# Which engine does which split: part of the GpSimd work of a two-layer encoder given to VectorE and ScalarE

## The chip, the core and the metric

The kernel runs on one core of a Trainium2 chip. Its engines are TensorE (PE in the profile), VectorE (DVE), ScalarE (ACT), GpSimd (POOL) and SyncE (SP), which issues all the DMAs here. The metric is the device time of one execution in microseconds (us).

## The reference

A prompt of 1024 tokens and a sample of 512 tokens, each of width 1024, go through two layers. Layer 0 projects x into eight pieces. Two of them (xa, za) go through a pooling mixer with windows of 2, 4, 8 and 16 tokens. The others go through a convolution and, per head, through a chunkwise mLSTM in both directions. Layer 1 is attention with grouped keys and an output gate. Each layer ends with an output projection and a layer norm.

```python
# pooling mixer, group g of 128 channels, window w
mean = (cs[hi] - cs[lo]) / cnt                       # cs: running sum over time
mixed = einsum('btc,cd->btd', mean - xa, w_pool[g]);  out_a = mixed * pool_scale * silu(za)
# mLSTM, one chunk of 128 tokens, per head and direction
s   = (q @ k.T) * exp(dmat - m_row)                  # dmat: masked decays
num = s @ v + ex * (C @ q);   den = s.sum(-1) + ex * (n @ q)
h   = num / max(abs(den), exp(-m_row))
C   = decay * C + einsum('s,sv,sk->vk', ws, v, k)    # ws: weight of each token for the state
n   = decay * n + einsum('s,sk->k', ws, k)
# layer 1
o = softmax(q @ k.T * scale) @ v;  x = layer_norm(ALPHA * x + (o * silu(z)) @ w_out)
```

All is in float32.

## The kernel before

**Split products.** A float32 matrix product is made of three matmuls in a shorter type (float32r). Each operand is split into a high part `h` (the value rounded to that type) and a low part `l` (the value less `h`), and PE sums h x h, h x l and l x h. The high part is a copy or cast, by ScalarE (`hi_act`, line 96) or by GpSimd (`hi_pool`, line 93). The low part is a subtraction, by VectorE (`lo_dve`, line 99) or, in `split_light`, by GpSimd (line 103). Since these helpers record the instructions, many groups of the profile carry lines 93, 96, 99 and 103, and the tile's name tells what is split.

**Order.** The program is written as Python generators that are merged, and the framework then orders each engine's instructions by a simulated timeline. Every engine, and SP's queue of DMAs, works its list off in order. So a store that waits for its data holds back every DMA behind it in SP's queue.

**Layer 0's token projections** (`layer0`, lines 285 to 338). Two pieces of the weights (`wt`) are multiplied with the tokens, for three groups of 512 tokens: the prompt's two and the sample's one. Each group makes four tiles `ev`, which ScalarE copies out of PSUM (line 322, or with a tanh in line 325) into a ring `th` of the pool `st` (three buffers), and which SP then stores. Between the groups runs `weight_sums`: for ten blocks of layer 1's weights, four pieces are loaded into a ring `sr` of eight buffers, four differences are made (line 1120), two on GpSimd and two on VectorE, each in the place of one of its inputs, and the differences are stored. They are read again in layer 1. Two rounds of table products (line 1132) follow. Here too stand the gates: VectorE's scans over time (lines 467 to 470), and transposes of the gates on PE into tiles `ct` (`gate_cols`, line 507), which need PSUM banks that the copies of `ev` set free.

**The heads** (from line 339). Periods overlap for the heads of prompt and sample: `early` prepares a head, `chains` runs the state from chunk to chunk, `head_fin` finishes it, and `fill` runs the projections of the heads to come (`proj_g`, with weights from `wunit`). 16 blocks of weights in two units each are split for the prompt; the split weights are stored and loaded again for the sample. In `wunit` the flag `wlight` chooses `split_light`. In `early`, line 643 multiplies the values `v` with the state's token weights `ws` into `vw`, which is split into `vwh` and `vwl` for the matmuls `U`. GpSimd also masks the decays (line 606) and takes the powers for the norms (line 195). `pool_mix` builds a window's sum by doublings (line 817), one to four additions in a row. `out_weights` splits the sixteen tiles of layer 0's output weights (`wo0`), every other one by `split_light`.

**After the heads** come layer 0's output projection with its norm (`mid`), layer 1's projections and attention, with a hand-written order on PE.

Of the kernel before, what the change touches and what calls it, by code (L numbers as in the profile page):

```python
# [10 lines left out]
F32 = mybir.dt.float32  # L11
F32R = mybir.dt.float32r
AF = mybir.ActivationFunctionType
ALU = mybir.AluOpType
# [4 lines left out]
P = 128  # L19
# [37 lines left out]
class Kern:  # L57
# [217 lines left out]
    def layer0(self, seqs):  # L275
# [4 lines left out]
        with ExitStack() as ctx:  # L280
# [4 lines left out]
            with ExitStack() as c1:  # L285
                mp = c1.enter_context(tc.tile_pool(name="mm0", bufs=4, space=PSUM, reuse_waits="tile"))
                mq = c1.enter_context(tc.tile_pool(name="ms0", bufs=4, space=PSUM, reuse_waits="tile"))
                gp = c1.enter_context(tc.tile_pool(name="gate", bufs=1, reuse_waits="tile"))
                xq = c1.enter_context(tc.tile_pool(name="x0b", bufs=1, reuse_waits="tile"))
                st = c1.enter_context(tc.tile_pool(name="st0", bufs=3, reuse_waits="tile"))  # L290
                self.wp = c1.enter_context(tc.tile_pool(name="w0", bufs=1, reuse_waits="tile"))
                self.wbufs, self.rbufs = 10, 4
                presums = self.weight_sums(st)
                self.gate_places(gp)

                acc = mq.tile([P, 512], F32, tag="ms", name="warm")
                for i in range(10):
                    self.mm(acc[:, 0:512], self.wgh[:, 0, :], self.wgh[:, 0:4, :], True, True)
                for piece in range(2):
                    units = []  # L300
                    for gi, (s, g) in enumerate(groups):
                        xh, xl = x0[s]
                        pool, tag = ((mp, "mm"), (mq, "ms"))[gi % 2]
                        acc = [pool.tile([P, 512], F32, tag=tag, name=f"t{s}{piece}{g}{i}") for i in range(4)]
                        for k in range(KD):
                            if gi == 0:
                                units.append(self.wunit(a["w0t"][piece, k], f"wt{piece}{k}"))
                            if piece == 0:
                                self.load_x(s, k, g, xh, xl, xp if s == first else xq, st)
                            elif gi and k == 3:  # L310
                                self.gate_cols(seqs[gi - 1], *gates[gi - 1], mq if pool is mp else mp, "ms" if pool is mp else "mm")
                            wh, wl = units[k]
                            for i in range(4):
                                c = slice(i * P, (i + 1) * P)
                                self.mm(acc[i], xh[k][g][:, c], wh, k == 0, False)
                                self.mm(acc[i], xh[k][g][:, c], wl, False, False)
                                self.mm(acc[i], xl[k][g][:, c], wh, False, k == KD - 1)
                        for i in range(4):
                            n = 4 * g + i
                            t = st.tile([P, 512], F32, tag="th", name=f"ev{s}{piece}{n}")  # L320
                            if piece == 0:
                                nc.scalar.copy(t, acc[i])
                                self.load(self.vd[s][n], t)
                            else:
                                nc.scalar.activation(t, acc[i], AF.Tanh, scale=0.5)
                                self.load(self.thd[s][n], t)
                        if piece == 0 and gi == 0:
                            self.consts0a()
                            self.gate_weights(gp)
                            self.consts0b(mq)  # L330
                        if piece or gi:
                            for _ in range(4 if piece and gi == len(groups) - 1 else 2):
                                next(presums, None)
                    if piece == 0:
                        gates = [self.gates(s, *x0[s], gp, mq) for s in seqs]
                        for k in range(KD):
                            for x, X in enumerate(x0[seqs[1]]):
                                self.load(self.xsd[k, x], X[k][0].bitcast(F32))
# [4 lines left out]
            self.rings = {"mm": (pp, 2), "me": (pp, 3), "mx": (pp, 1), "mc": (pp, 2)}  # L343
            self.wp = c2.enter_context(tc.tile_pool(name="w1", bufs=1, reuse_waits="tile"))
            self.wbufs, self.rbufs = 4, 2
            self.wlight = True
            hp = self.hp = c2.enter_context(tc.tile_pool(name="hd", bufs=1, reuse_waits="tile"))
            self.xbt, self.state = {}, {}

# [34 lines left out]
            for i in range(-1, n + 1):  # L384
# [16 lines left out]
                    ts = self.mid_early[i + 2 - len(plan)]  # L401
                    jobs.append((chain(*[self.mid_tile(t) for t in ts]), 16 * len(ts)))
                merge(*jobs)
            self.wlight = False

    def head_plan(self, seqs):

# [143 lines left out]
    def early(self, s, h, hp, hf):  # L551
# [25 lines left out]
        for g in range(NG):  # L577
# [3 lines left out]
            kl = hp.tile([P, 512], F32R, tag="kl", name=f"kl{s}{h}{g}")  # L581
            N, keep = vs[g]
            qh, ql = keep[:, 0, :], keep[:, 1, :]
            self.hi_pool(kh, xc)
            self.lo_dve(kl, xc, kh)
            yield
            wh, wl = self.wsm["wqk"]
# [31 lines left out]
            nc.gpsimd.memset(v[:, :, P:130], 1.0)  # L619
            vh = hf.tile([P, 4, 130], F32R, tag="vh", name=f"vh{s}{h}{g}", bufs=1)  # L620
            vl = hf.tile([P, 4, P], F32R, tag="vl", name=f"vl{s}{h}{g}", bufs=1)
            self.hi_pool(vh, v)
            self.lo_dve(vl, v[:, :, 0:P], vh[:, :, 0:P])
            yield
            ps = self.bank("me", f"S{s}{h}{g}")
# [12 lines left out]
            for i in range(0, 4, 2):  # L638
# [1 line left out]
                vw = hf.tile([P, 2, 2, 130], F32, tag="vw", name=f"vw{s}{h}{g}{i}")  # L640
                vb = v[:, i:i + 2, :].unsqueeze(2).to_broadcast([P, 2, 2, 130])
                ws = col["ws"][:, 4 * g + i:4 * g + i + 2, :, h:h + 1].to_broadcast([P, 2, 2, 130])
                nc.gpsimd.tensor_tensor(out=vw, in0=vb, in1=ws, op=ALU.mult)
                vwh = hf.tile([P, 2, 2, 130], F32R, tag="vwh", name=f"vwh{s}{h}{g}{i}")
                vwl = hf.tile([P, 2, 2, 130], F32R, tag="vwl", name=f"vwl{s}{h}{g}{i}")
                self.hi_act(vwh, vw)
# [153 lines left out]
    def pool_mix(self, s, gi, hp):  # L800
# [10 lines left out]
        for g in range(NG):  # L811
            gc = slice(g * 512, (g + 1) * 512)
            cur, ln, step = xa[:, g * 512:g * 512 + 512 + w - 1], 512 + w - 1, 1
            for i in range(gi + 1):
                nxt = hp.tile([P, 526], F32, tag=f"y{i % 2}", name=f"y{s}{gi}{g}{i}")
                ln -= step
                nc.gpsimd.tensor_tensor(out=nxt[:, 0:ln], in0=cur[:, 0:ln], in1=cur[:, step:step + ln], op=ALU.add)
                cur, step = nxt, step * 2
            if g == 0:
                nc.vector.tensor_tensor(out=cur[:, 0:left], in0=cur[:, 0:left], in1=self.edge[:, gi, 0:left], op=ALU.mult)  # L820
# [5 lines left out]
            sz = self.load_z(s, gi, g, hp)  # L826
            qh = hp.tile([P, 512], F32R, tag="zs", name=f"plh{s}{gi}{g}", bufs=2)
            ql = hp.tile([P, 512], F32R, tag="zs", name=f"pll{s}{gi}{g}", bufs=2)
            self.hi_pool(qh, cur[:, 0:512])
            self.lo_dve(ql, cur[:, 0:512], qh)  # L830
            yield
            ps = self.bank("mx", f"mx{s}{gi}{g}")
# [21 lines left out]
    def out_weights(self, wn, half):  # L854

        wh, wl = [], []
        for k in range(KD):
            l = self.x0p.tile([P, 512], F32R, tag=f"xl{k}{1 - half}", name=f"{wn}l{half}{k}")
            h = self.x0p.tile([P, 512], F32R, tag=f"xh{k}{1 - half}", name=f"{wn}h{half}{k}")
            raw = self.hp.tile([P, 512], F32, tag="zs", name=f"{wn}r{half}{k}", bufs=2)  # L860
            self.load(raw, self.a[wn][k, :, half * 512:(half + 1) * 512])
            if k % 2:
                self.split_light(h, l, raw)
            else:
                self.hi_act(h, raw)
                self.lo_dve(l, raw, h)
            wh.append(h)
            wl.append(l)
        self.wo[half] = (wh, wl)
# [237 lines left out]
    def weight_sums(self, pool):  # L1107

        nc = self.nc
        for kind, n in (("q", 4), ("z", 4), ("kv", 2)):
            for k in range(n):
                r = {}
                for h, j in ((0, 0), (0, 1), (1, 1), (1, 0)):
                    t = r[h, j] = pool.tile([P, 512], F32, tag="sr", name=f"sr{kind}{k}{h}{j}", bufs=8)
                    self.load(t.rearrange("p (k n) -> p k n", k=2) if kind == "kv" else t, self.piece(kind, k, h, j))
                for o, e, x, y, d in ((0, nc.gpsimd, (0, 1), (0, 0), (0, 0)), (2, nc.vector, (1, 1), (0, 1), (0, 1)),
                                      (1, nc.gpsimd, (1, 1), (0, 0), (1, 1)), (3, nc.vector, (1, 1), (1, 0), (1, 0))):
                    e.tensor_tensor(out=r[d], in0=r[x], in1=r[y], op=ALU.subtract)  # L1120
                    self.load(self.sums[kind][k, o], r[d])
                yield
        g = pool.tile([P, 4, P], F32, tag="sr", name="srg", bufs=8)
        self.load(g.rearrange("p a f -> p (a f)"), self.a["g4"].partition_broadcast(P))
        for h in range(2):
            ns = slice(4 * h, 4 * h + 4)
            for i, n in enumerate(("cos", "sin")):
                t = pool.tile([P, 4, P], F32, tag="sr", name=f"srt{h}{n}", bufs=8)
                self.load(t, self.a[n][:, ns, :])
                for w in range(2):  # L1130
                    o = pool.tile([P, 4, P], F32, tag="sr", name=f"sro{h}{n}{w}", bufs=8) if w == 0 else t
                    nc.vector.tensor_tensor(out=o, in0=t, in1=g[:, 2 * w + i:2 * w + i + 1, :].to_broadcast([P, 4, P]), op=ALU.mult)
                    self.load(self.tabd[w][i][:, ns, :], o)
            yield
# [519 lines left out]
```

## Time and profile before

| | |
|---|---|
| median of three runs | 1479.44 us (1478.56 to 1479.59) |
| the profiled execution | 1477.55 us, of which the span of the instructions is 1475.8 us |
| granted PE clock over the span | 0.99 |
| bytes read and written in HBM | 155.94 and 86.03 MB |

A row of windows gives a stretch, and for each engine its busy time and how many instructions ran in it; then the granted clock of PE as a share of the full one, the busy share of the 16 DMA engines, and GB/s. A row of waits names who waited for whom, the sum, how often, and the longest, all in us. A row of a group gives the instruction's line, engine, operation, `out<-in`, shapes and count, then its busy time in us and the mean of one in ns, then the idle time of the engine ahead of it and what ended that. A row in time begins with the start and the duration in us. Names ending in p belong to the prompt, those ending in s to the sample. The stages by time: token projections 0 to 165 us, heads 165 to about 640, output projection to 711, layer 1 to the end.

### The profile page before, as it was taken

The page shows a single profiled execution, that of the slowest core. Times are in us where ns is not written, and L with a number is a line of the kernel's source. Part 1 is how long each engine was busy: PE and PEld are TensorE (multiplying, and loading weights), DVE is VectorE, ACT ScalarE, POOL GpSimd, SP SyncE. Part 2 cuts the span into 40 slices and gives each one's busy share as a digit, 9 for nine tenths or more (in the row PEclk, how much of TensorE's full clock was granted, in tenths as well). Part 3 has the DMA queues.
Part 4 walks back from the last instruction along what each step waited for, and adds up shares of the span by engine and source line. Part 5 has one row for each costly group of instructions (what it writes and reads, how often), then busy time and mean ns, then how long its engine had stood idle before and what let it go on. Part 6 is the DMA issues. An engine that isn't in the chain of part 4 may idle for free.

```text
span 1475.8 us, 21781 instructions
## 1 busy us (share of the span) xinstructions
PE 1435.2 (97%) x7190; PEld 1189.3 (81%) x7190; DVE 1012.5 (69%) x1976; ACT 738.4 (50%) x1666; POOL 609.0 (41%) x616
## 2 busy tenths in 40 slices
PE   9998999999999999999999999999999999999997
PEld 7876888878787788788888789888878888888886
DVE  6584156585777878877779548555677777777675
ACT  3341355454545555445346545557755555555551
POOL 5431334353542333659426002432345545444641
PEclk9998999999999999999999999999999999999999
DMA  9976564555597776545554876345321111111311
GB/s 311 396 282 235 190 201 139 204 176 178 160 310 245 233 229 208 181 147 185 172 167 145 271 226 234 121 136 157 114 72 58 57 51 37 43 58 58 100 51 57
DMA packets 181586, 243.42 MB, mean 165 GB/s; under 512 B 14673, under 2 KB 90193, under 8 KB 181473
## 3 DMA queue, kind: packets, MB, share of 16 engines
q1 hardware_dynamic: 181472, 242.03, 49.7%
q8 instruction: 57, 0.93, 0.3%
q14 instruction: 57, 0.46, 0.1%
HBM read 155.94 MB, written 86.03 MB: 164 GB/s over the span
## 4 chain that ended last, share of the span: by engine, by line
PE 65%; DVE 13%; DMA 12%; issue 4%; ACT 3%; POOL 2%; SPq 1%; DVEq 0%; ACTq 0%; POOLq 0%
PE Sp L106 6%; PE Op L106 6%; PE o1p L106 6%; PE ptp L1442 4%; PE o1s L106 3%; PE qs L106 3%; PE o0s L106 3%; PE z L106 3%; PE zp L106 3%; PE o0p L106 3%; PE xbp L106 2%; PE kvs L106 2%; PE ts L106 1%; PE Ss L106 1%; PE z4P L106 1%
## 5 line engine op out<-in xcount | busy, mean ns | idle before, releaser
L1420 POOL TENSOR_SCALAR prp<-prp,smp 128x1024 f32<-128x1024 f32 x64 | 73.3, 1145 | 137.8 <-DVE smp L1419 112.7
L96 ACT CAST pwp<-ptp 128x512 fp32r<-128x512 f32 x128 | 74.8, 585 | 92.1 <-PE ptp L1442 91.4
L106 PE MATMUL Op<-pwp,Vhp 128*128 128x512 f32 x256 | 109.0, 426 | 0.6 <-DVE pwp L99 0.6
L99 DVE TENSOR_TENSOR pwp<-ptp,pwp 128x512 fp32r<-128x512 f32 x128 | 87.2, 682 | 22.9 <-ACT pwp L96 22.7
L1415 ACT ACTIVATE prp<-Sp,nbp,rqp 128x1024 f32<-128x1024 f32 (+1 forms) x68 | 78.8, 1159 | 21.6 <-DVE nbp L1412 15.8
L1407 DVE TENSOR_REDUCE nbp<-Sp 128x1 f32<-128x1024 f32 (+1 forms) x68 | 78.4, 1153 | 11.8 <-PE Sp L106 11.7
L1442 PEld LDWEIGHTS ptp<-idn,prp 128*128 128x128 f32 x512 | 63.5, 140 | 20.0 <-DVE pwp L99 1.9
L1442 PE MATMUL ptp<-idn,prp 128*128 128x128 f32 x512 | 77.0, 272 | 2.0 <-POOL prp L1420 1.4
L106 PEld LDWEIGHTS Op<-pwp,Vhp 128*128 128x128 f32 x256 | 48.3, 189 | 8.0 <-DVE pwp L99 1.0
L106 PE MATMUL tp<-wt_l,xhp 128*128 128x512 f32 x128 | 51.2, 404 | 0.0
L106 PE MATMUL tp<-wt_h,xlp 128*128 128x512 f32 x128 | 51.1, 403 | 0.0
L106 PE MATMUL o0p<-wo0l,ah0p 128*128 128x512 f32 x128 | 50.8, 399 | 0.2 <-DVE wo0l L99 0.2
L106 PE MATMUL o0p<-wo0h,ah0p 128*128 128x512 f32 x128 | 50.6, 397 | 0.2 <-ACT wo0h L96 0.2
L106 PE MATMUL tp<-wt_h,xhp 128*128 128x512 f32 x128 | 50.7, 403 | 0.0
L106 PE MATMUL o0p<-wo0h,al0p 128*128 128x512 f32 x128 | 50.3, 394 | 0.0
L106 PE MATMUL Op<-pwp,Vlp 128*128 128x512 f32 x128 | 50.1, 391 | 0.0
L1067 POOL TENSOR_TENSOR rskp<-sskp,mhalf 128x2 f32<-128x2 f32 x8 | 7.0, 879 | 100.2 <-DVE sskp L1063 100.2
L106 PE MATMUL Sp<-Khp,qhp 128*128 128x512 f32 x128 | 41.9, 403 | 0.0
L106 PE MATMUL o1p<-wo,ah1p 128*128 128x512 f32 x128 | 40.7, 399 | 0.0
L106 PE MATMUL Sp<-Klp,qhp 128*128 128x512 f32 x128 | 40.7, 393 | 0.0
L106 PE MATMUL Sp<-Khp,qlp 128*128 128x512 f32 x128 | 40.4, 391 | 0.0
L699 DVE SCALAR_TENSOR_TENSOR Usp<-Usp,decbp 128x130 f32<-128x130 f32 x48 | 22.2, 462 | 25.8 <-ACT Usp L656 25.2
(1150 smaller groups left out, 4999.5 us busy)
## 6 DMA issues: line engine op xcount, KB each, us to landing
wt_r<-w0t SPq DMA_DIRECT2D x16, 256.0 KB, 5.2
xrp<-xT_p SPq DMA_DIRECT2D x16, 256.0 KB, 5.4
srq<-w1q SPq DMA_DIRECT2D x16, 256.0 KB, 5.4
sum_q<-srq SPq DMA_DIRECT2D x16, 256.0 KB, 5.3
srz<-w1z SPq DMA_DIRECT2D x16, 256.0 KB, 5.1
sum_z<-srz SPq DMA_DIRECT2D x16, 256.0 KB, 4.8
wp<-rd_p SPq DMA_DIRECT2D x16, 256.0 KB, 4.9
z_p<-zsp SPq DMA_DIRECT2D x16, 256.0 KB, 3.2
```

Source lines behind the costliest of these rows:

```text
L96: self.nc.scalar.copy(out, in_)
L99: self.nc.vector.tensor_tensor(out=out, in0=in_, in1=hi.bitcast(F32), op=ALU.subtract)
L106: self.nc.tensor.matmul(out, lhsT=lhsT, rhs=rhs, start=start, stop=stop)
L699: nc.vector.scalar_tensor_tensor(out=U[:, i, :], in0=U[:, i + o, :], scalar=dec[:, 4 * d + h, n:n + 1], in1=U[:, i, :], op0=ALU.mult, op1= ...
L1067: nc.gpsimd.tensor_tensor(out=rs[:, 0:nh], in0=ss[:, 0:nh], in1=self.mhalf[:, 0:nh], op=ALU.pow)
L1407: nc.vector.tensor_reduce(out=nb[:, i:i + 1], in_=b, op=ALU.max, axis=AX.X, negate=True)
L1415: nc.scalar.activation(pr[:, i * W:(i + 1) * W], b, AF.Exp, bias=nb[:, 0:1], scale=rq, accum_out=sm[:, i:i + 1])
L1420: nc.gpsimd.tensor_scalar(pr, pr, sm, 0.0, ALU.mult, ALU.add)
L1442: nc.tensor.transpose(pt[:, h * P:(h + 1) * P], prs[h][:, c * P:(c + 1) * P], self.idn)
```

## The change

Four things. In layer 0 the ring `th` gets four buffers, the ring `sr` seven, and all four differences of a weight block are made by VectorE. In the heads the weights' low parts go from GpSimd to VectorE (`wlight` stays off, and `hi_w` is ScalarE, which makes the high parts as before). The weighted values `vw` and the windows' sums go from GpSimd to VectorE; so do the low parts of every other tile of `wo0`. The high parts of the keys' input (`kh`), the values (`vh`) and the pooled tiles (`plh`) go from GpSimd to ScalarE. GpSimd keeps the masks, the powers and the memsets in the heads. `hi_w` is set back after the heads, so what follows is not edited.

```diff
@@ layer0
-  t = st.tile([P, 512], F32, tag="th", name=f"ev{s}{piece}{n}")
+  t = st.tile([P, 512], F32, tag="th", name=f"ev{s}{piece}{n}", bufs=4)
...
-  self.wlight = True
+  self.hi_w = self.hi_act
...
-  self.wlight = False
+  self.hi_w = self.hi_pool
@@ early
-  self.hi_pool(kh, xc)
+  self.hi_act(kh, xc)
...
-  self.hi_pool(vh, v)
+  self.hi_act(vh, v)
...
-  nc.gpsimd.tensor_tensor(out=vw, in0=vb, in1=ws, op=ALU.mult)
+  nc.vector.tensor_tensor(out=vw, in0=vb, in1=ws, op=ALU.mult)
@@ pool_mix
-  nc.gpsimd.tensor_tensor(out=nxt[:, 0:ln], in0=cur[:, 0:ln], in1=cur[:, step:step + ln], op=ALU.add)
+  nc.vector.tensor_tensor(out=nxt[:, 0:ln], in0=cur[:, 0:ln], in1=cur[:, step:step + ln], op=ALU.add)
...
-  self.hi_pool(qh, cur[:, 0:512])
+  self.hi_act(qh, cur[:, 0:512])
@@ out_weights
-  if k % 2:
-      self.split_light(h, l, raw)
-  else:
-      self.hi_act(h, raw)
-      self.lo_dve(l, raw, h)
+  self.hi_act(h, raw)
+  self.lo_dve(l, raw, h)
@@ weight_sums: every tile of the ring "sr"
-  bufs=8
+  bufs=7
...
-  for o, e, x, y, d in ((0, nc.gpsimd, (0, 1), (0, 0), (0, 0)), (2, nc.vector, (1, 1), (0, 1), (0, 1)),
-                        (1, nc.gpsimd, (1, 1), (0, 0), (1, 1)), (3, nc.vector, (1, 1), (1, 0), (1, 0))):
-      e.tensor_tensor(out=r[d], in0=r[x], in1=r[y], op=ALU.subtract)
+  for o, x, y, d in ((0, (0, 1), (0, 0), (0, 0)), (2, (1, 1), (0, 1), (0, 1)),
+                     (1, (1, 1), (0, 0), (1, 1)), (3, (1, 1), (1, 0), (1, 0))):
+      nc.vector.tensor_tensor(out=r[d], in0=r[x], in1=r[y], op=ALU.subtract)
```

More of the change, by code (lines that the diff above doesn't have):

```diff
@@ L1115, in weight_sums @@
                 for h, j in ((0, 0), (0, 1), (1, 1), (1, 0)):
-                    t = r[h, j] = pool.tile([P, 512], F32, tag="sr", name=f"sr{kind}{k}{h}{j}", bufs=8)
+                    t = r[h, j] = pool.tile([P, 512], F32, tag="sr", name=f"sr{kind}{k}{h}{j}", bufs=7)
                     self.load(t.rearrange("p (k n) -> p k n", k=2) if kind == "kv" else t, self.piece(kind, k, h, j))
-                for o, e, x, y, d in ((0, nc.gpsimd, (0, 1), (0, 0), (0, 0)), (2, nc.vector, (1, 1), (0, 1), (0, 1)),
-                                      (1, nc.gpsimd, (1, 1), (0, 0), (1, 1)), (3, nc.vector, (1, 1), (1, 0), (1, 0))):
-                    e.tensor_tensor(out=r[d], in0=r[x], in1=r[y], op=ALU.subtract)
+                for o, x, y, d in ((0, (0, 1), (0, 0), (0, 0)), (2, (1, 1), (0, 1), (0, 1)),
+                                   (1, (1, 1), (0, 0), (1, 1)), (3, (1, 1), (1, 0), (1, 0))):
+                    nc.vector.tensor_tensor(out=r[d], in0=r[x], in1=r[y], op=ALU.subtract)
                     self.load(self.sums[kind][k, o], r[d])
                 yield
-        g = pool.tile([P, 4, P], F32, tag="sr", name="srg", bufs=8)
+        g = pool.tile([P, 4, P], F32, tag="sr", name="srg", bufs=7)
         self.load(g.rearrange("p a f -> p (a f)"), self.a["g4"].partition_broadcast(P))
@@ L1127, in weight_sums @@
             for i, n in enumerate(("cos", "sin")):
-                t = pool.tile([P, 4, P], F32, tag="sr", name=f"srt{h}{n}", bufs=8)
+                t = pool.tile([P, 4, P], F32, tag="sr", name=f"srt{h}{n}", bufs=7)
                 self.load(t, self.a[n][:, ns, :])
                 for w in range(2):
-                    o = pool.tile([P, 4, P], F32, tag="sr", name=f"sro{h}{n}{w}", bufs=8) if w == 0 else t
+                    o = pool.tile([P, 4, P], F32, tag="sr", name=f"sro{h}{n}{w}", bufs=7) if w == 0 else t
                     nc.vector.tensor_tensor(out=o, in0=t, in1=g[:, 2 * w + i:2 * w + i + 1, :].to_broadcast([P, 4, P]), op=ALU.mult)
```

## The prediction, made before the changed kernel ran

> **What bounds the kernel now.** I read the first part of the page first, then windows of stages, then who made TensorE (PE) wait, then the chain of waits and single engines in time.
>
> ```profile
> span 1475.8 us, 21781 instructions
> PE 1435.2 (97%) x7190; PEld 1189.3 (81%) x7190; DVE 1012.5 (69%) x1976; ACT 738.4 (50%) x1666; POOL 609.0 (41%) x616
> ```
>
> PE is busy for 97% of the span, so the most that any change off PE can return is what PE loses: 1475.8 - 1435.2 = 40.6 us of idleness, plus the time at a reduced clock. POOL is the least loaded engine, and taking work off it is worth nothing by itself. The question is only which PE waits end on work that this change moves.
>
> ```profile
> core 0: us, PE busy (x) PEld busy (x) DVE busy (x) ACT busy (x) POOL busy (x), PEclk, DMA share, GB/s
> 126.00:133.00 7.00, 0.32 (x7) 0.20 (x5) 1.43 (x3) 0.66 (x4) 0.00 (x0) 0.71 0.84 314
> 134.00:139.20 5.20, 5.20 (x13) 4.13 (x13) 2.77 (x4) 0.29 (x2) 0.00 (x0) 0.50 0.92 327
> 139.20:144.40 5.20, 5.20 (x24) 4.12 (x23) 1.38 (x2) 1.80 (x3) 0.00 (x0) 1.00 0.30 112
> 323.50:330.30 6.80, 6.58 (x19) 5.42 (x20) 4.33 (x10) 5.00 (x15) 3.52 (x5) 0.50 0.89 327
> 484.00:490.80 6.80, 6.14 (x15) 4.88 (x16) 5.70 (x12) 5.32 (x12) 3.42 (x3) 0.50 0.48 147
> 165.00:640.00 475.00, 456.35 (x2351) 382.81 (x2350) 339.77 (x734) 238.51 (x573) 195.77 (x222) 0.99 0.62 202
> 400.00:640.00 240.00, 229.54 (x1182) 191.28 (x1181) 186.60 (x443) 119.31 (x284) 95.97 (x105) 0.99 0.71 230
> ```
>
> Two losses lie where the change works. **Layer 0's token projections (0 to 165 us):** one stall at 126, in which PE works 0.32 of 7.00 us, so 6.7 us are lost; and behind it PE runs at a granted clock of 0.50, so that 13 matmuls go into 5.2 us where the next 5.2 us take 24: another 5.2 x (1 - 13/24) = 2.4 us. Together 9.1 us. **The heads (165 to 640):** 475 - 456.35 = 18.7 us idle, and two stretches of 6.8 us at half clock that cost up to 3.4 us each, some 25 us in all. Work after 640 is not edited; I leave it as it is.
>
> What ends the stall at 126, from the chain of waits, then ScalarE (ACT) and the DMA queue in time:
>
> ```profile
> 119.68 1.30 POOL srkv L1120
> 121.00 1.77 DVE srkv L1120
> ...
> 126.63 5.61 DMA thd_p<-evp
> ...
> 133.00 1.07 PE ctpen L507 x8
> ```
>
> ```profile
> 119.61 2.00 ACT L325 ACTIVATE evp<-tp 128x512 f32<-128x512 f32 x3 [0.98 <-PE tp L106]
> 132.34 0.60 ACT L325 ACTIVATE evp<-tp 128x512 f32<-128x512 f32 x1 [10.74 <-DMA thd_p<-evp]
> 142.08 2.00 ACT L325 ACTIVATE evp<-tp 128x512 f32<-128x512 f32 x3 [7.68 <-issue]
> ```
>
> ```profile
> 119.34 4.25 SPq L90 DMA_DIRECT2D sum_kv<-srkv  x5
> 126.63 2.29 SPq L90 DMA_DIRECT2D thd_p<-evp  x3
> ```
>
> Four tiles are evacuated into a ring of three. The first three copies are done by 121.6. The fourth waits 10.7 us until the first copy's store has landed, because that store sits behind the stores of the weight sums in SP's queue, and these wait for sums that POOL and VectorE (DVE) make in turn. PE's transposes wait for the bank that the fourth copy frees.
>
> PE's waits in the heads, longest first, and two DVE instructions ahead of the two longest, each beside the POOL instruction that runs with it:
>
> ```profile
> PE Up L106 <- DVE vwlp L99: 2.8, 1, 2.8
> PE Ss L106 <- DVE keeps L99: 2.2, 1, 2.2
> PE hTs L772 <- ACT ths L768: 2.2, 1, 2.2
> PE Ap L106 <- ACT Np L664: 1.1, 2, 0.9
> PE xbs L106 <- ACT xbps L524: 0.9, 1, 0.9
> ```
>
> ```profile
> 318.41 1.50 POOL L103 TENSOR_TENSOR xbp3u_l<-xbp3u_r,xbp3u_h 128x512 fp32r<-128x512 f32 x1
> 318.69 1.76 DVE L778 TENSOR_TENSOR xcrp<-xcrp,szp 128x512 f32<-128x512 f32 x1
> 474.86 1.31 POOL L103 TENSOR_TENSOR wo0l<-wo0r,wo0h 128x512 fp32r<-128x512 f32 x1
> 475.05 1.67 DVE L758 SCALAR_TENSOR_TENSOR thp<-thp,Np 128x512 f32<-128x512 f32 x1 [0.65 <-DMA thp<-thd_p]
> ```
>
> The 2.8 us (with 0.9 right after it) precede the half clock at 323.5; the 2.2 and 0.9 us precede that at 484. So each event costs about 3.5 + 3.4 = 7 us. Ahead of each, a DVE instruction took 1.7 us instead of some 0.7 while POOL made a weight's low part, and DVE's queue behind it came late by 1 us. Both POOL instructions are ones that move.
>
> **The change part by part.** Prices:
>
> ```profile
> L103 POOL TENSOR_TENSOR wo0l<-wo0r,wo0h 128x512 fp32r<-128x512 f32 x8 | 11.5, 1440 | 11.2 <-ACT wo0h L96 10.2 <-PE Bs L106 0.8 <-DVE Uss L699 0.2
> L643 POOL TENSOR_TENSOR vwp<-vrp,colpws 128x520 f32<-128x520 f32 x16 | 18.9, 1183 | 20.9 <-DVE vwlp L99 18.1 <-DMA act_p<-xcrp 1.5 <-PE xbp L106 1.3
> L1120 POOL TENSOR_TENSOR srz<-srz,srz 128x512 f32<-128x512 f32 x8 | 11.9, 1498 | 19.3 <-DVE srz L1120 13.6 <-DMA srz<-w1z 2.9 <-issue 2.2
> L1120 DVE TENSOR_TENSOR srz<-srz,srz 128x512 f32<-128x512 f32 x8 | 6.9, 861 | 2.6 <-POOL srz L1120 2.6
> L99 DVE TENSOR_TENSOR klp<-xcp,khp 128x512 fp32r<-128x512 f32 x8 | 5.4, 680 | 0.5 <-POOL xbpp L526 0.5
> L99 DVE TENSOR_TENSOR plp<-wp,php 128x512 fp32r<-128x512 f32 x16 | 16.9, 1064 | 1.0 <-ACT php L96 0.8
> L96 ACT CAST php<-wp 128x512 fp32r<-128x512 f32 x16 | 9.8, 620 | 15.9 <-DVE wp L634 15.9
> PE ts L106 <- DVE xls L99: 1.3, 1, 1.3
> ```
>
> *Evacuation ring of four in layer 0.* The fourth copy needs no landed store, so it runs at 121.7, right behind the third, and PE's transposes at 126 find their bank free. Between 0 (the stall is set by something else) and 9.1. The next round of copies began at 142.1 and will begin near 133; the stores of the first round, issued from 126.6 to 128.9 and 5.6 us long, land by 134.5, so at worst a copy waits 1.5 us. I take 9.1: the row shows a free engine waiting for nothing but this buffer.
>
> *Weight sums all on DVE.* 10 blocks x 2 = 20 sums move. On POOL they took 1.5 us; on DVE between 0.68 (the low part klp, same size) and 0.86 us: 13.6 to 17.2 us of DVE work, cheaper because the pair of engines no longer alternates. PE waits for DVE only once in this stage, 1.3 us for xls. A sum or two queued ahead of it adds up to 1.4 us; the wait also could vanish. Bounds -1.3 to +1.4, taken as 0. *Sum ring of seven instead of eight:* each block's fourth load must now wait for the first store of the block before, and what is queued behind it on SP (other loads and the stores of copies) waits too. One landing is 5.6 us; the upper bound is one such wait reaching PE, +5.6, the lower 0. I take 0, as PE's only wait for SP's order was the one above.
>
> *Low parts of weights.* 16 blocks x 2 units + 4 in each of two halves of the output weights = 40 subtractions from POOL (1.44 us) to DVE (0.68): 27 us on DVE. The pair of split instructions ahead of a projection shortens by 0.76 us; no PE wait above names these weights, so that itself is worth 0.
>
> *Weighted values.* 24 multiplies, POOL 1.18 to DVE about 0.68: 16 us on DVE, the chain to vwlp 0.5 us shorter. *Pool sums.* Prompt 2 x (1+2+3+4) = 20, sample 10: 30 additions, 20 us on DVE. They feed the pool mixer, which PE hardly waits for. *High parts of keys, values and pooled tiles.* 3 x 12 = 36 casts to ACT at 0.62: 22 us on ACT, which has 475 - 238.5 us free. A cast in front of a copy that PE waits for can cost 0.62; taken as 0.
>
> So DVE gets 27 + 16 + 20 = 63 us in the heads, against 135 us idle. It gets back what POOL took from it: low parts of one shape cost 0.68 (klp) or 1.06 us (plp), 0.38 apart. If a sixth of DVE's 734 instructions lose that, 47 us come back (an estimate; between 16 x 0.38 = 6 us from plp alone and the 196 us that POOL is busy there). Net DVE load: 340 + 63 - 47 = 356 of 475, 75% after 72%: no new bound on average.
>
> What the heads' PE waits do: at the two events, 1.0 us of blocking goes, and a low part of 0.68 may come in its place. I take one event of 7 us as shortened to 2 us without half clock, and the rest of the 25 us as staying, partly at other places: -5. Between -16 (both events gone, 14, and the 2.2 us of hTs, whose row scaling comes from DVE) and +14 (two new events).
>
> On what decides an event: after idle stretches of 2.8 + 0.9 and 2.2 + 0.6 + 0.9 us the clock was halved, after 2.2 us alone (PE hTs) it was not. The Trainium skill, "TensorE: Matmul & The Clock Gate" (Part 1), puts the limit at one idle window of about 3.4 us that runs freely; by it, taking 1 us off the 2.8 us wait is enough to keep the clock in most positions of the window, and the heads would gain both half clocks, 6.8 us, in place of the 5 that I take.
>
> **Sum.** -9.1 - 5 = -14.1 us. The profiled execution took 1477.55 (1475.8 span and 1.75 around it), 1.9 below the median of three runs, 1479.4. Against that median: 1465.3. Differences of under 0.2% (3 us) count as no change here.
>
> **Rivals.**
> *The heads give nothing.* DVE's returned time and its new work cancel, and waits only change places: 1479.4 - 9.1 = 1470. For it: the two sums above, 63 against 47, are close. The Trainium skill, "Perfetto Trace Analysis" (Optimizing Scalar/DVE Operations), says that shifting work between GpSimd and VectorE might not help since they share a read port, and advises moving work off a saturated VectorE, not on to it; plp beside klp shows the sharing. Against it: what moves is the half that blocks the other.
> *The heads gain most:* both events and the wait of hTs vanish: 1479.4 - 9.1 - 16 = 1454, or 1459 with two thirds of it. Against: three of the five rows of waits are ACT's, which gets work.
> *Slower: DVE becomes late in the crowded second half.* From 400 to 640 it is busy 186.6 us; 8 low parts, 9 weighted values and 18 pool sums start there, and 35 at 0.68 add 24: 211 of 240, 88%, if nothing comes back. Each wait of over 3 us then also costs a half clock, 7 us. The sign turns at two new events with neither old one gone: 1479.4 - 9.1 + 14 = 1484. For it: 88% in an engine that works in order. Against: POOL's lock is on the trace.
> *The ring doesn't do it:* the stall stays or comes back at another wait for SP (sum ring of seven): 1479.4 - 0 to -3 = 1478.
>
> **Chances.** Forecast (1461 to 1469) 0.40; heads nothing (1469 to 1473) 0.22; heads most (1450 to 1461) 0.14; slower (1480 to 1492) 0.12; ring fails (1475 to 1481) 0.12. Faster by over 3 us: 0.40 + 0.22 + 0.14 + a third of the last = 0.80; same 0.08; slower 0.12. The range 1456 to 1480 leaves out the slower case and half of "heads most". The likeliest case's own range is 1461 to 1469.
>
> **What would show it.** In the profile after: no wait of PE ctpen for evp and no half clock near 130; the layer's second round of copies begins near 133 instead of 142.1; DVE's plp falls from 1.06 towards 0.68 us; POOL is busy well below 100 us in the heads instead of 196; half-clock stretches in the heads one or none. It is wrong if the ctpen wait survives, if plp stays at 1.06, or if PE's idle time in the heads exceeds 28 us.

## The result, and the profile after

The changed kernel ran in 1470.21 us, the median of three runs (1467.61 to 1470.90); the kernel before in 1479.44. The ratio is 0.9932, with a 95% interval of 0.9913 to 0.9950. In the experiments below it ran again, on another chip, at 0.9905 (0.9887 to 0.9923) of the kernel before. It is 0.7 to 1.0% faster. The profiled execution took 1467.61 us, of which 1465.9 are its span. From here `after` is the changed kernel, `before` the kernel before.

The page's first part and the windows of `after`, to be read beside those of `before`:

```profile
span 1465.9 us, 21754 instructions
PE 1432.6 (98%) x7190; PEld 1189.5 (81%) x7190; DVE 1024.0 (70%) x2090; ACT 753.7 (51%) x1702; POOL 431.8 (29%) x466
```

```profile
core 0: us, PE busy (x) PEld busy (x) DVE busy (x) ACT busy (x) POOL busy (x), PEclk, DMA share, GB/s
126.00:133.00 7.00, 7.00 (x32) 5.65 (x31) 3.11 (x5) 2.12 (x4) 0.00 (x0) 1.00 0.71 214
165.00:640.00 475.00, 460.42 (x2380) 389.11 (x2379) 352.60 (x840) 259.58 (x620) 59.90 (x101) 0.98 0.62 202
446.70:453.50 6.80, 6.80 (x24) 5.94 (x24) 3.34 (x8) 5.65 (x16) 1.21 (x2) 0.50 0.94 307
508.10:514.90 6.80, 5.17 (x19) 4.55 (x20) 5.58 (x9) 6.71 (x20) 1.27 (x2) 0.50 0.27 92
596.90:600.30 3.40, 3.24 (x11) 2.46 (x12) 0.57 (x2) 3.40 (x8) 1.36 (x2) 0.50 0.44 148
700.00:735.00 35.00, 31.23 (x131) 23.64 (x130) 23.38 (x38) 16.83 (x46) 11.30 (x10) 0.98 0.63 211
```

POOL works 177 us less, and PE's stall at 126 is gone. But the half clock has not left the heads: it stands at three other places. And 700 to 735, the entry of layer 1, now loses 3.8 us; in `before` PE was busy for all of these 35 us.

Where the time went is read from two instructions that every version has: PE's first product of the heads (xbp) and its first product of layer 1 (qP1i). The rows are groups of one form; behind the shortest, median and longest duration in ns stand the first and the last start in us. First `before`, then `after`:

```profile
L106 PE MATMUL xbp<-xhp,xbp0u_h x16: 389/389/397, 167.1 to 177.3; 128*128 128x512 f32 x16
L106 PE MATMUL qP1i<-kv0h,A11h x4: 389/392/393, 711.3 to 719.7; 128*128 128x512 f32 x4
```

```profile
L106 PE MATMUL xbp<-xhp,xbp0u_h x16: 389/389/497, 157.4 to 167.8; 128*128 128x512 f32 x16
L106 PE MATMUL qP1i<-kv0h,A11h x4: 388/391/393, 696.1 to 704.4; 128*128 128x512 f32 x4
```

So layer 0's projections gained 167.1 - 157.4 = 9.7 us. The heads with the output projection gained (711.3 - 167.1) - (696.1 - 157.4) = 5.5. What lies behind lost (1465.9 - 696.1) - (1475.8 - 711.3) = 5.3. The sum is the 9.9 us between the two spans. The same three stages of every kernel, from the same two rows and the span (us), with the ratio to the kernel before on the same chip:

| kernel | layer 0 | heads | rest | ratio (95%) |
|---|---|---|---|---|
| before | 167.1 | 544.2 | 764.5 | 1 |
| after, first profile | 157.4 | 538.7 | 769.8 | 0.9932 (0.9913 to 0.9950) |
| after again (e0) | 156.4 | 535.2 | 768.1 | 0.9905 (0.9887 to 0.9923) |
| e1 rings of layer 0 alone | 164.0 | 549.4 | 768.3 | 0.9987 (0.9974 to 1.0000) |
| e2 weight sums alone | 160.8 | 544.3 | 765.5 | 0.9943 (0.9928 to 0.9958) |
| e8 layer 0's part alone | 158.1 | 548.1 | 764.3 | 0.9949 (0.9931 to 0.9968) |
| e3 heads' part alone | 166.9 | 530.2 | 768.3 | 0.9949 (0.9932 to 0.9966) |
| e10 layer 0, weighted values and sums | 157.8 | 539.3 | 769.2 | 0.9950 (0.9932 to 0.9967) |
| e4 after, low parts on POOL | 157.8 | 541.7 | 764.7 | 0.9905 (0.9887 to 0.9922) |
| e6 after, high parts on POOL | 158.2 | 528.8 | 766.7 | 0.9850 (0.9830 to 0.9871) |
| e7 after, norm on DVE | 158.8 | 538.1 | 764.5 | 0.9903 (0.9888 to 0.9919) |
| e11 e6 and e7 | 157.1 | 530.3 | 765.7 | 0.9851 (0.9835 to 0.9867) |
| e12 after, two mask buffers | 156.6 | 527.8 | 766.4 | 0.9831 (0.9815 to 0.9847) |
| e13 e12, e7 and wo0's high parts on POOL | 157.2 | 533.9 | 766.6 | 0.9883 (0.9863 to 0.9902) |

The stages are those of one profiled run, which can lie several us off its kernel's median: e1's is the slowest of its twelve runs (1483.5 us, median 1477.4), e3's the fastest of its six (1467.1, median 1472.2). Two profiles of `after` differ by 3.5 us in the heads, so smaller differences there say nothing. The ratio is of medians: of three runs in the first row of `after`, of four to twelve in the rows below it.

### The profile page after: what moved, and what is told of

It is laid out like the page before. It is cut to its first block, busy times and chain, and to the rows that moved or that the text cites. A ratio compares the mean times of both kernels' runs of the same rounds, so it can differ in the third digit from the quotient of the medians.

```text
span 1465.9 us, 21754 instructions
## 1 busy us (share of the span) xinstructions
PE 1432.6 (98%) x7190; PEld 1189.5 (81%) x7190; DVE 1024.0 (70%) x2090; ACT 753.7 (51%) x1702; POOL 431.8 (29%) x466
## 4 chain that ended last, share of the span: by engine, by line
PE 79%; DVE 7%; DMA 7%; ACT 2%; issue 2%; POOL 1%; SPq 0%; DVEq 0%; ACTq 0%; POOLq 0%
PE Sp L106 6%; PE tp L106 6%; PE Op L106 6%; PE o1p L106 6%; PE zp L106 5%; PE ptp L1439 4%; PE o0p L106 3%; PE o1s L106 3%; PE qs L106 3%; PE xap L106 3%; PE z L106 3%; PE ts L106 3%; PE xbp L106 2%; PE kvs L106 2%; PE Ss L106 1%
## 5 line engine op out<-in xcount | busy, mean ns | idle before, releaser
L606 POOL TENSOR_SCALAR_AFFINE_SELECT wp<-wp 128x512 f32<-128x512 f32 x16 | 10.2, 640 | 134.1 <-ACT wp L603 107.1
L1416 DVE RECIPROCAL smp<-smp 128x1 f32<-128x1 f32 x64 | 10.5, 164 | 38.5 <-ACT prp L1412 38.4
```

The costliest lines, as they stand in the source:

```text
L606: nc.gpsimd.affine_select(out=wv, in_=wv, pattern=[[0, 4], [sg, P]], compare_op=ALU.is_ge, fill=0.0, base=0, channel_multiplier=-sg)
L1416: nc.vector.reciprocal(out=sm, in_=sm)
```

## The experiments

**What ended the stall of layer 0.** The prediction gave it to the ring of copies.

e1, the rings alone:

```diff
-  t = st.tile([P, 512], F32, tag="th", name=f"ev{s}{piece}{n}")
+  t = st.tile([P, 512], F32, tag="th", name=f"ev{s}{piece}{n}", bufs=4)
...  every tile of the ring "sr"
-  bufs=8
+  bufs=7
```

> The kernel before with the two rings of layer 0 alone: four buffers for the copies of ev, seven for the weight sums, which GpSimd and VectorE still make in turn; the heads as before. Theory (the stall at 126 us was a full ring of copies and nothing else): no wait of ctpen there, the second round of copies near 133 us, no half clock behind it, and the whole of layer 0's 9 us: 1470.3 us, 1468 to 1472. Rival (the copies' stores stand behind the sums' stores in SP's queue, and sums made in turn by two engines keep them late, so that the stall returns one tile later or at the shorter sum ring): a wait of over 3 us in 126 to 145 us and 1475 to 1479 us.

Measured: 0.9987 (1477.4 us, in the rival's range), so the rings alone bring next to nothing. PE's waits, and ScalarE in time:

```profile
PE ctpex L507 <- ACT evp L325: 6.4, 1, 6.4
```

```profile
108.59 1.30 ACT L325 ACTIVATE evp<-tp 128x512 f32<-128x512 f32 x2 [0.37 <-PE tp L106]
122.75 0.21 ACT L489 ACTIVATE decs<-decs 40x4 f32<-40x4 f32 x1 [12.86 <-DVE decs L488]
122.86 1.06 ACT L325 ACTIVATE evp<-tp 128x512 f32<-128x512 f32 x2
```

The stall is there, 6.4 us long, nine us earlier, and it has another cause. No copy waits for a store any more. But the third and fourth copy now stand behind the gate's `decs` in ScalarE's queue, and that waits 12.9 us for VectorE's chain of gates. By the chain of waits, a sum on GpSimd (2.29 us from 107.8) is part of that chain: its store goes out through SP ahead of the gates' own load (`decbp`), and VectorE's scans go on at 112.9. No run has the ring of four without the ring of seven, so what each of the two did here is not separated.

e2, the sums alone: `weight_sums` as in the change, with rings of three and eight.

> The kernel before with the weight sums by VectorE alone; both rings of layer 0 and the heads as before. Theory (the ring of copies is the cause): the fourth copy still waits for the landing of the first one's store, the wait shortens by 2 us at most since each pair of sums is made sooner, and the half clock stays: 1477.5 to 1480 us. Rival (the slow alternation of the two engines was the cause): the stores come 4 us or more earlier, the wait falls under 3 us, the half clock goes with it: 1470 to 1474 us.

Measured: 0.9943 (1471.0 us, in the rival's range). PE's wait in 100 to 165 us, the window of the old stall, PE's transposes ctpen, and the fourth copy:

```profile
PE xbp L106 <- ACT evs L325: 4.1, 1, 4.1
```

```profile
126.00:133.00 7.00, 7.00 (x36) 5.73 (x36) 2.33 (x4) 2.15 (x7) 0.00 (x0) 1.00 0.98 379
```

```profile
L507 PE MATMUL ctpen<-idn,mp x8: 229/230/253, 125.8 to 126.3; 40*128 40x40 f32 x8
```

```profile
130.06 0.60 ACT L325 ACTIVATE evp<-tp 128x512 f32<-128x512 f32 x1 [7.09 <-DMA thd_p<-evp]
```

The fourth copy still waits 7.1 us for a store to land, as the theory said; PE does not wait with it, as it did not say. In this program the order of each engine's work is planned anew after every edit: `ctpen` runs at 125.8, ahead of the fourth copy at 130.1, while in `before` it stood behind it. What the ring of three costs now comes 30 us later, 4.1 us for `evs`.

e8, both: rings of four and seven with the sums on VectorE, heads as before.

> The layer 0 part of the change alone: sums by VectorE, rings of four and seven; the heads as before. Theory (sums by VectorE end the stall at 126 us, and the fourth buffer for the copies then shortens the next wait, that of xbp for evs at 156 us, which was 4.1 us with three buffers): layer 0 loses 5 us less than with the sums alone, 1467 to 1470.5 us, so that the heads' part adds 0 to 2 us to it in the whole change. Rival (the two parts add up: the heads' part alone gave 5.7 us, so this one gives 9.2 less 5.7): 1473 to 1476 us.

Measured: 0.9949 (1471.8 us, between the two ranges), the same as the sums alone. The wait for `evs` fell from 4.1 to 1.7 us, and layer 0 takes 158.1 us. In this stage's own time the parts nearly add up: the rings alone take 3.1 us off it (e1), the sums 6.3 (e2), both 9.0. The sums on VectorE are the larger part; the 2.7 us that the rings add to them were not passed on by the heads in this profile (548.1 after 544.3).

**What the heads' part is worth alone.** e3 is the change with layer 0 as before.

> The change without its layer 0 part: rings of three and eight, sums made in turn by GpSimd and VectorE, and the heads as changed. Theory (the heads are worth about 5 us, and up to 5.8 of that is given back at layer 1's entry, where PE now comes to its first products before the norm's stores and the loads behind them): the stall at 126 us is there as before, heads lose 4 to 7 us less than before, PE waits at qP2i and qP6i after about 715 us: 1474 to 1479 us. Rival 1 (the heads' part is worth the whole 9 us and layer 0's gain is lost later): 1470 us. Rival 2 (nothing is given back, the entry of layer 1 differs by chance): 1472 to 1474.5 us with no wait at qP6i.

Measured: 0.9949 (1472.2 us). The old stall is there (layer 0 takes 166.9 us). The heads take 530.2 us, 14 less than in `before`, in a profile of the fastest of its runs; the rest gives back 3.8. None of the three expectations fits: the time is that of rival 2, but qP6i waits (1.7 us). The two halves of the change gain 0.5% each alone and 0.7 to 1.0% together.

**Which part of the heads.** With the weighted values and sums on VectorE and layer 0 as changed, e10, e4 and e6 put the low and high parts on the one engine or the other.

```diff
 e4 and e10: low parts of the weights as before
-  self.hi_w = self.hi_act
+  self.wlight = True
... and in out_weights every other tile
+  if k % 2: self.split_light(h, l, raw)
 e6 and e10: high parts as before
-  self.hi_act(kh, xc);  self.hi_act(vh, v);  self.hi_act(qh, cur[:, 0:512])
+  self.hi_pool(kh, xc); self.hi_pool(vh, v); self.hi_pool(qh, cur[:, 0:512])
```

> The changed kernel itself once more, beside the three variants that follow, on their chip. Both theories: 0.993 of the kernel before, 1467 to 1471 us. Its profile, compared with the first one of the same program, tells which of PE's waits in the heads come back and which are of one run.

> The changed kernel with the low parts of the weights (two units of 16 blocks, and every other tile of wo0) back on GpSimd. Theory (the blocking of VectorE by these subtractions made the two waits with half clocks at 319 and 479 us): they come back, 3 to 7 us slower than the changed kernel, 1473 to 1477 us. Rival (with the weighted values and sums gone from GpSimd the subtractions find another moment): within 1.5 us of the changed kernel.

> The changed kernel with the high parts of keys, values and pooled tiles (36 casts) back on GpSimd. Theory (the waits that the changed kernel has in the heads, Bp for the copy Uss at 444 us and Us for vwhs at 505 us, stand behind an instruction of ScalarE that waits for a load, 3.3 and 3.7 us, and not behind the casts that it was given): they stay, 1469 to 1473 us, no gain. Rival (ScalarE's 22 us of casts make them): both waits fall below 1 us and the half clocks go, 1462 to 1467 us.

> Layer 0 as changed; in the heads only the weighted values and the windows' sums go to VectorE, while GpSimd keeps the low parts of the weights and the high parts of keys, values and pooled tiles. Theory (of what moved in the heads, the weighted values and sums alone gain, the low parts are worth nothing, and the casts on ScalarE cost 9 us): as the changed kernel with the casts back on GpSimd, 0.985 of the kernel before, 1454 to 1460 us. Rival (the low parts gain only while GpSimd has the casts to make): 3 to 9 us slower than that, 1460 to 1467 us.

Measured: e0 0.9905; e4 0.9905, no difference, as its rival said; e6 0.9850, 8 to 9 us better than `after` on the same chip, against the theory; e10 0.9950, worse than all three and slower than both of its ranges. In the heads the parts have no price of their own. Low parts on VectorE took 10.5 us from the heads with the casts on POOL (e10 to e6). With the casts on ScalarE it was 3 to 6.5 us (e4 to the two profiles of `after`), little more than those two differ, and the stage behind gave it back: 764.7 us in e4, 768 to 770 in `after`. Casts on ScalarE cost 6 to 10 us in the heads beside the low parts (e6 to `after`). Without them (e10 to e4) the 2.4 us in the heads are too few to tell, while the whole time falls by 0.45%; in these two profiles that lies behind the heads (769.2 to 764.7).

What PE waited for changed with all of them. Summed over 165 to 640 us, PE waited 10.0 us for VectorE and 7.8 for ScalarE in `before`, and 9.9 and 8.5 in e8, which leaves the heads as they were. In `after` the two sums are 1.6 and 12.6, in e4 2.7 and 11.9, in e10 2.9 and 12.2, in e6 0.6 and 8.4. So the waits for VectorE go even where the low parts stay on GpSimd (e4 and e10). What the four kernels share in the heads is the weighted values and the sums on VectorE. The waits for ScalarE are what is left. Each sum is that of one profiled run.

Why the casts cost is on ScalarE's line. `after`, then e10, then e6, the activations L603 on a mask tile `ws`, with what stands around them:

```profile
507.61 1.28 ACT L603 ACTIVATE ws<-ws,colsa 128x128 f32<-128x128 f32 x4 [3.68 <-DMA ws<-rd_s]
508.79 0.35 ACT L656 COPY Uss<-Us 128x260 f32<-128x260 f32 x1
509.05 0.62 ACT L96 CAST vwhs<-vws 128x520 fp32r<-128x520 f32 x1
```

```profile
510.67 1.28 ACT L603 ACTIVATE ws<-ws,colsa 128x128 f32<-128x128 f32 x4 [2.67 <-DMA ws<-rd_s]
511.85 0.35 ACT L656 COPY Uss<-Us 128x260 f32<-128x260 f32 x1
512.11 0.62 ACT L96 CAST vwhs<-vws 128x520 fp32r<-128x520 f32 x1
```

```profile
505.63 0.38 ACT L656 COPY Uss<-Us 128x260 f32<-128x260 f32 x1 [0.38 <-PE Us L106]
505.90 0.63 ACT L96 CAST vwhs<-vws 128x520 fp32r<-128x520 f32 x1
...
509.99 1.28 ACT L603 ACTIVATE ws<-ws,colsa 128x128 f32<-128x128 f32 x4 [1.87 <-DMA ws<-rd_s]
```

PE's waits in the heads of `after`:

```profile
PE Us L106 <- ACT vwhs L96: 4.3, 1, 4.3
PE hTs L772 <- ACT ths L768: 2.5, 1, 2.5
PE zp L106 <- ACT xbpp L524: 2.1, 1, 2.1
PE Bp L106 <- ACT Uss L656: 1.9, 1, 1.9
```

In `after` ScalarE is idle for 3.7 us before `ws`, whose load has not landed, and the copy and the cast that PE needs stand behind it: 4.3 us of PE, and a half clock of 6.8. In e10 the casts are on POOL, and the wait is there too (2.7 us, of which PE pays 2.3). In e6 the plan puts `ws` behind them, and PE waits for next to nothing (0.2 us from 495 to 520). e3 has the order of `after` here, with the casts on ScalarE; its load was late by 1.7 us only, PE waited 2.3 us, and the clock stayed full. So a queue in order waits for a load, and the plan decides what stands behind it. Both readings were left: the load or the casts' own time. e12 decides.

e12 gives the mask tile a second buffer, so that its load goes out a group earlier:

```diff
-  w = hp.tile([P, 2, 512], F32, tag="w", name=f"w{s}{h}{g}")
+  self.wn = 1 - getattr(self, "wn", 1)
+  w = (hp, hf)[self.wn].tile([P, 2, 512], F32, tag=("w", "w2")[self.wn], name=f"w{s}{h}{g}")
```

> The changed kernel in which the tile w (masks and decays of a head's group, loaded from rd) has two buffers in turn instead of one, so that its load can go out a group earlier; the casts stay on ScalarE. Theory (ScalarE's in-order queue waits for that load, 3.7 us at 504 us in the first profile, with the copy Uss and the cast vwhs behind it): that wait and PE's 4 us for vwhs go, with the half clock behind it: 4 to 8 us below the changed kernel, 0.985 to 0.988 of the kernel before. Rival (the casts' own time on ScalarE makes it): PE's wait stays over 2 us, no gain over 1.5 us.

Measured: 0.9831 (0.9815 to 0.9847), 11 to 15 us below `after` on the ratios, with the casts still on ScalarE. It is the lowest ratio of all, though its interval overlaps those of e6 and e11. The same place:

```profile
502.01 1.65 ACT L769 ACTIVATE thp<-thp,nmp,r0p_rs 128x128 f32<-128x128 f32 x4
503.56 0.35 ACT L657 COPY Uss<-Us 128x260 f32<-128x260 f32 x1
503.82 0.62 ACT L96 CAST vwhs<-vws 128x520 fp32r<-128x520 f32 x1
```

Copy and cast follow without a wait; from 495 to 560 us no wait of PE is left. The last mask load went out at 474.5 instead of 501.4. The activations on it still wait 3.5 us for a load, but they stand at 478.8 instead of 507.6, and PE, busy throughout from 474 to 484, does not wait for what is behind them. The late load ahead of copy and cast made PE's wait, not the casts' own time. The gain is larger than the 4 to 8 us that were expected: PE's wait of 4.3 us and up to 3.4 us for the half clock behind it make 7.7, and the rest is not explained.

**The entry of layer 1.** PE's waits of `after` there, one row each of VectorE and POOL ahead of them, and the DMA queue:

```profile
PE qP6i L106 <- DVE u L1168: 2.0, 1, 2.0
PE qP2i L106 <- DVE w1q7l L99: 0.9, 1, 0.9
PE qP6i L106 <- ACT whq L96: 0.8, 1, 0.8
```

```profile
705.83 1.78 DVE L99 TENSOR_TENSOR w1q6l<-q_r,w1q6h 128x512 fp32r<-128x512 f32 x1
705.63 3.13 POOL L927 TENSOR_TENSOR xr0s<-xr0s,ln 128x512 f32<-128x512 f32 x2
709.34 1.49 SPq L90 DMA_DIRECT2D x_s<-xr0s  x3
713.39 0.32 SPq L90 DMA_DIRECT2D rt0qp<-tab  x1
714.24 0.42 SPq L90 DMA_DIRECT2D q0t_r<-sum_q  x1
```

The low part w1q6l takes 1.78 us beside POOL's norm instead of the 0.68 of such an instruction alone. The norm's last stores leave at 709.3, and the loads that layer 1 needs wait behind them until 714. PE came 15 us earlier than in `before`, these two loads only 8 and 9 us (there they left at 721.5 and 723.6).

e7: `out_norm` takes its way through VectorE for the last two tiles instead of the last:

```diff
-  hp, t + 1 == len(self.mid_tiles))
+  hp, t + 2 >= len(self.mid_tiles))
```

> The changed kernel, in which the last but one tile of layer 0's norm takes the way by VectorE that the last one takes already, so that GpSimd multiplies nothing beside the last tile's norm. Theory (PE's waits at the entry of layer 1, 3.8 us and a half clock of 2 us behind them, come from the norm's tail, in which VectorE instructions took 1.4 to 1.8 us instead of 0.7 beside GpSimd's, so that the last stores and the loads behind them are late): x_s is stored 2 us or more earlier than 709.3, the half clock near 733 us is gone, and the time is 1465 to 1468 us, that is 2 to 5 below the changed kernel's 1470.2. Rival (these waits are set by the loads and splits of the weights, not by the norm): the waits of qP6i stay, 1469 to 1472 us.

> The changed kernel with the casts back on GpSimd and the last but one tile of layer 0's norm on VectorE: both edits that gained alone. Theory (they lie in different stages, the heads and the entry of layer 1): at most the 6 us that the norm gave before, less what the casts' return already took from the entry's waits (5.8 to 2.8 us there): 2 to 4 us below the kernel with the casts alone, 0.982 to 0.984 of the kernel before, 1450 to 1456 us. Rival (the norm's gain was a gain of the entry's waits that the casts' return has taken): no difference from 0.985.

The one wait of PE left in 690 to 750 us of e7, and its stores and loads:

```profile
PE Tqp L1232 <- POOL t0qp L1072: 0.7, 1, 0.7
```

```profile
707.10 0.98 SPq L90 DMA_DIRECT2D x_s<-xr0s  x2
708.19 0.39 SPq L90 DMA_DIRECT2D rt0qp<-tab  x1
710.25 0.42 SPq L90 DMA_DIRECT2D q0t_r<-sum_q  x1
```

The mechanism is as stated: the loads leave 4 to 5 us earlier, and the stage takes 764.5 us, as in `before`, instead of 768 to 770. In the whole time it can't be told: 0.9903 lies with the two ratios of `after`, and e11 with e6 (0.9851, 0.9850). Its gain of 4 to 5 us is seen in the stage of this profile, not in the time; e11 gains 1.0 us there over e6, and e4 takes 764.7 us without this edit.

e13 is e12 with e7's edit and wo0's high parts by `hi_pool`:

> The kernel with two mask buffers (0.983 of the kernel before), and two more edits in other places: the high parts of the sixteen wo0 tiles by GpSimd instead of ScalarE, and the last but one tile of the norm on VectorE. Theory (ScalarE's queue waits for loads, and what PE needs stands behind; at 444 us it waited 3.8 us for wo0r with the copy Uss behind): PE's wait of 2.4 us there and its half clock go, 2 to 4 us, and the entry of layer 1 loses 1 us less: 0.979 to 0.982 of the kernel before, 1446 to 1451 us. Rival (GpSimd's casts take longer and VectorE's low parts of wo0 come later, so that the products with wo0 wait in their turn; the entry is set by something else by now): 0.982 to 0.987, waits of o0p on wo0h or wo0l over 1 us near 580 us.

Measured: 0.9883, worse than e12 by 8 us and outside both ranges. Neither expectation names why: o0p has no wait. ScalarE no longer waits for wo0's loads, but for the next load in its queue:

```profile
447.75 0.72 ACT L777 ACTIVATE xcrp<-xcrp,vec 128x512 f32<-128x512 f32 x1 [4.67 <-DMA xcrp<-xcd_p]
466.45 0.72 ACT L777 ACTIVATE xcrp<-xcrp,vec 128x512 f32<-128x512 f32 x1 [6.32 <-DMA xcrp<-xcd_p]
467.08 0.57 ACT L524 COPY xbps<-xbs 128x512 f32<-128x512 f32 x1
```

PE waits 1.8 us for a cast behind the first of them and 1.6 us for that last copy, and the clock is halved twice, 3.4 us each, at 450 and 467; e12 has one such half clock there, at 448.5. To take one such instruction out of the queue brought the next one forward here; to let its load go out earlier, as in e12, took PE's wait away. e13 holds two edits more than e12, and their shares are not told apart.

## Why the prediction was right, and what in it was not

*Layer 0, -9.1.* Right in size, 9.7, and by luck, since the change held a second part that did most of the work. The signs came: no wait of ctpen, no half clock, the second round of copies at 130.6 us (near 133 was said). The cause was wrong. The prediction gave 9.1 to the ring and 0 to the sums; alone the rings gave nothing that can be told in the whole time (0.9987, with 3.1 us in the stage of its slowest run) and the sums 8.4 us (0.57% of 1477.9, with 6.3 in the stage). The step that failed is "the row shows a free engine waiting for nothing but this buffer": true of the order in `before`, but an edit makes a new order, and in that one the copies stood behind the gate's chain. The ring of seven was put at 0. In e1 GpSimd waits 12.2 us for two loads of weight pieces into it (srkv), for which it does not wait in `before`; no wait of PE names that ring.

*Loads of the engines.* Right: VectorE was forecast at 356 us in the heads and took 352.6 from 165 to 640 us, ScalarE at 238.5 + 22 = 260.5 and took 259.6, POOL at well below 100 and took 59.9. But `after` is 10 to 15 us ahead of `before` there. Over the same work, 155.3 to 624.8 us, they took 343.7, 253.9 and 55.8; so 340 + 63 - 344 = 59 us of VectorE came back where 47 were said. The prompt's low part plp has a median of 684 ns and none over 694:

```profile
L99 DVE TENSOR_TENSOR plp<-wp,php x16: 680/684/694, 191.3 to 412.3; 128x512 fp32r<-128x512 f32 x16
```

The rule that was weighed as a rival, that moving work between GpSimd and VectorE might not help (the Trainium skill, "Perfetto Trace Analysis", Optimizing Scalar/DVE Operations), held in one arrangement of the heads and not in the other: low parts moved from GpSimd to VectorE gain 1.0% from e10 to e6, and nothing from e4 to e0.

*Heads, -5.* Near in size, 5.5 and 9.0 us in two profiles, and right that waits change places; that the size came out is partly luck. The prediction shortened one event and let the rest stay. In `after` neither of the two old waits is left (Up for vwlp, 2.8 us, and Ss for keeps, 2.2), which alone is 14 us by its own price, and new waits for ScalarE with half clocks took much of it back. That GpSimd's low parts caused the old waits is not shown: with them back on GpSimd (e4) Up waits 0.4 us for vwlp and Ss not at all, and the time is that of `after`. The sign "half-clock stretches one or none" failed: the first profile has three, the second two. "High parts: taken as 0" failed: beside the low parts on VectorE they cost 8 to 9 us, by e12 mainly because in that plan a wait for a load stands ahead of what PE needs. And the heads are held by loads that land late in ScalarE's queue, not by VectorE's blocking alone; no step of the prediction had that. Its five rows of waits, three of them ScalarE's, are not the five longest either: the same view has 1.5 us for keepp (ScalarE), 1.3 for clp and 1.2 for zss (both VectorE) ahead of the last two.

*"Work after 640 is not edited; I leave it as it is."* Failed: the stage behind lost 5.3 us (3.6 in the second profile), since PE arrives 15 us earlier and the loads behind the norm only 8 to 9. This takes the profiled gain from 15.2 to 9.9, and with it the median from the 1465 that was forecast to 1470. On the second chip the ratio of 0.9905 is 14 us, the size forecast, again with this loss in it.

The rivals: the heads did give something, though the total of the first runs is that of "heads give nothing", 1470. "Ring fails" (1478) is what e1 shows of the rings, 1477.4, and the sums made up for it.

What stays open: why casts on ScalarE gain without the low parts (e10 to e4, in the whole time) and cost with them, beyond that the order changes; which of the weighted values and the sums takes VectorE's waits away; why e12 gains more than the wait that it removes; and how much of each difference between two plans is chance. Each of these kernels is another plan.

## What to carry to other kernels

An engine's load and the price of one instruction say little where each engine works a list in order: ask for every wait of the critical engine which instruction stands at the head of the list that feeds it, and whether that one waits for a load. An earlier load (a second buffer) can then be worth more than a shorter instruction; here one buffer gave about as much as the whole change, 0.7 to 1.0%. Where a scheduler plans the order anew, a part of an edit may have no price of its own, as in the heads here, so parts are judged by running them in combination, and the stage behind a gain is looked at first, since work that was hidden until now is met earlier.

## What the runs showed of the hardware that was not expected

The clock was halved after short waits. PE waited 1.9 us at 444; it was busy for 1.54 of the 3.40 us up to 446.7 and then had 6.8 us at half clock. And the same wait can cost or not. PE's wait for `ths` near 595 us took 2.5 us in `after` and in e3. Here are windows of 3.4 us, laid on the steps at which each profile's clock changes: two of `after`, then two of e3.

```profile
443.30:446.70 3.40, 1.54 (x10) 1.05 (x9) 2.61 (x9) 0.89 (x2) 0.16 (x1) 1.00 0.82 257
593.50:596.90 3.40, 1.04 (x8) 0.71 (x6) 3.37 (x14) 0.39 (x1) 1.53 (x2) 1.00 0.84 293
```

```profile
593.20:596.60 3.40, 2.00 (x12) 1.47 (x11) 3.37 (x15) 0.47 (x1) 1.04 (x2) 1.00 0.65 208
596.60:600.00 3.40, 2.21 (x11) 1.48 (x12) 1.35 (x5) 2.81 (x6) 0.87 (x2) 1.00 0.64 257
```

In `after` the wait fell into one such stretch, which left PE 1.04 us busy, and 3.4 us of half clock followed (596.9 above). In e3 it fell across two, with 2.00 and 2.21 us busy, and none did. The busy time of such a stretch draws no sharp line: 1.54 us in `after` and 1.92 in `before` (480.6 to 484.0) were followed by a half clock, 1.55 in e12 (168.6 to 172.0) was not. The Trainium skill, "TensorE: Matmul & The Clock Gate" (Part 1), has a window of about 3.4 us that runs freely; the stretches of 3.4 and 6.8 us agree with it, while an idle window in full was not needed here. This may be one reason why one program scatters: `after` ran from 1461.4 to 1467.9 us on its second chip. Another may be when loads land: the wait of 1.9 us for `Uss` in its first profile isn't in its second, where ScalarE's waits for wo0's loads sum to 14.3 us instead of 19.2.
